# The last pass's inverse deviation: a table value with a Newton step on ScalarE, or a power on GpSimd

## The chip, the cores and the metric

The kernel runs on one core of a Trainium2 chip. A core has a matrix engine (TensorE, PE in the profile; its weight loads are PEld), a vector engine (VectorE, DVE), a scalar engine with function tables (ScalarE, ACT), a general engine (GpSimd, POOL), and a queue engine that issues DMAs (SyncE, SP). Each runs its own instruction stream in order; semaphores tie the streams together. On-chip memory is SBUF, with 128 partitions; matmul results land in PSUM banks. The metric is the device time of one execution, in microseconds (us).

## The reference

One layer of a hybrid decoder trunk over 1024 tokens (plus 16 prepended ones) of width 1024: input projections, a convolution branch and a windowed attention branch, a gated merge, a layer norm, and then a convolutional feed-forward block with a second layer norm. Only its end matters here:

```python
def layer_norm(x, g, b):
    xf = x.astype(jnp.float32)
    mu = xf.mean(-1, keepdims=True)
    var = jnp.square(xf - mu).mean(-1, keepdims=True)
    return ((xf - mu) * lax.rsqrt(var + LN_EPS) * g + b).astype(x.dtype)
...
f = (jax.nn.gelu(g, approximate=False) * u) @ ffn_w_down
return layer_norm(DEEPNORM_ALPHA * h + f, ln2_g, ln2_b)
```

Every token (row) of the result needs the mean and the variance of its 1024 values, and one inverse deviation, 1/sqrt(var + 1e-5).

## The kernel before

The down projection is the last stage. Its output is 1024 tokens by 1024 columns, cut into eight row tiles of 128 tokens and two column halves of 512; matrix products are done in seven passes over half-size blocks, each pass accumulating four PSUM banks (`down`, L1735 and after). A pass's `done` function takes each finished bank into the row tiles `rows[i]` in SBUF. The first six passes finish row tiles 4 to 7 and the second halves of tiles 0 to 3. The seventh, `down(X, True, c11_, 5)` at L1876, finishes the first half of tiles 0 to 3, one tile after another: with `by_tile=5` all remaining operands of a tile are multiplied before the next tile's, so the tiles become ready one by one. Tile 3 comes in two parts of 256 columns, in two banks.

`c11_` (L1850) is what happens to each of these tiles. On VectorE: the bank is added to the row (L1858), the half's statistics are taken (L1859), and both halves' statistics are joined to a mean and a variance, `mv` (L246, in `ln_stats`). Then the inverse deviation `r_` is made. Then each of the row's two halves is centred and multiplied by the gain, `(r - mu) * g2` (L1865), and each half is scaled by the inverse deviation and shifted, `r * rs + b2` (L1867); behind each of these a store of 256 KB to the output is issued on SyncE's queue (L1868, through the helper at L113). L1865 does not need the inverse deviation; L1867 does.

The inverse deviation (L253 to L259) is made mainly on ScalarE: a table value of 1/sqrt(var + eps) (L253), its square (L257), that square times `t_` plus 1.5 (L258), and the product with the table value (L259): one Newton step. `t_` is -0.5 (var + eps), a small VectorE instruction (L256). The `pin` argument is given by `c11_` alone; every other user of `ln_stats` makes its Newton step on VectorE (L261 to L263).

The order of work is planned: the program is laid out with a simulated schedule and ranks, and `after(a, b)` fixes an order between two instructions of an engine by hand. `pin_tail` (L1845) strings all VectorE instructions of `c11_` in the written order, so that tile i's two L1867 stand before tile i+1's L1858. GpSimd and ScalarE instructions of the tail are not strung. GpSimd has one other instruction there, a copy of six columns of statistics for tile 3 (L1857).

The constants used are small tiles filled by VectorE at the start of the program: `eps` (L173), `half` and `three_half` (L226 and L227).

Of the kernel before, what the change touches and what calls it, by code (L numbers as in the profile page):

```python
# [23 lines left out]
F = mybir.dt.float32  # L24
R = mybir.dt.float32r
AF = mybir.ActivationFunctionType
OP = mybir.AluOpType
AX = mybir.AxisListType

P = 128  # L30
# [18 lines left out]
EPS = 1e-5  # L49
# [52 lines left out]
def tile_hybrid_layer(  # L102
# [3 lines left out]
    nc = tc.nc  # L106
# [15 lines left out]
    def after(ins, first):  # L122

        tc.add_manual_dep(ins.ins, first.ins.name, mybir.DependencyInfo(
            mybir.DependencyClass.NoSync, mybir.DependencyReason.SCHED_ONLY), reason="order of work")
# [10 lines left out]
    const = ctx.enter_context(tc.tile_pool(name="const", bufs=1, side="left"))  # L136
# [34 lines left out]
    eps = const.tile([P, 1], F, name="eps")  # L171
# [52 lines left out]
    half_2 = const.tile([P, 2], F, name="half")  # L224
    half_, three_half = (half_2[:, i:i + 1] for i in range(2))
    nc.vector.memset(half_, 0.5)  # L226
    nc.vector.memset(three_half, 1.5)  # L227
    nc.vector.memset(xm[:NMETA], 0.0)
    nsink = const.tile([P, NH], F, name="nsink")

    def ln_stats(srcs, pool=None, tag="", bufs=4, behind=None, half_stats=None, pin=None):

        pool = pool or small
        J = len(srcs)
        n = max(n for _, n in srcs)
        mv = pool.tile([P, J, 2], F, name="mv", tag="mv" + tag, bufs=bufs)
        if any(m < n for _, m in srcs):
            nc.vector.memset(mv, 1.0)
        for j, (src, m) in enumerate(srcs):
            st = half_stats or small.tile([P, 2, 6], F, name="st")  # L240
            for i in range(0 if half_stats is None else 2, 2):
                ins = nc.vector.bn_stats(st[:m, i, :], src[:, i * 512:(i + 1) * 512])
                if behind is not None:
                    after(ins, behind)
                    behind = None
            ins = nc.vector.bn_aggr(mv[:m, j], st[:m].rearrange("p a b -> p (a b)"))  # L246
            if pin:
                pin(ins)
        sd = pool.tile([P, 2, J], F, name="sd", tag="sd" + tag, bufs=bufs)
        t_, r_ = (sd[:n, i] for i in range(2))  # L250
        var = mv[:n, :, 1]

        nc.scalar.activation(r_, var, AF.Abs_reciprocal_sqrt, bias=eps[:n], scale=1.0)  # L253
        if pin:
            sq = pool.tile([P, J], F, name="sq")
            pin(nc.vector.tensor_scalar(t_, var, EPS, -0.5, OP.add, OP.mult))  # L256
            nc.scalar.activation(sq, r_, AF.Copy, scale=r_)  # L257
            nc.scalar.activation(sq, sq, AF.Identity, scale=t_, bias=three_half)  # L258
            nc.scalar.activation(r_, r_, AF.Copy, scale=sq)  # L259
            return [(mv[:m, j, 0:1], r_[:m, j:j + 1]) for j, (_, m) in enumerate(srcs)]  # L260
        nc.vector.scalar_tensor_tensor(t_, var, EPS, r_, OP.add, OP.mult)  # L261
        nc.vector.scalar_tensor_tensor(t_, t_, -0.5, r_, OP.mult, OP.mult)
        nc.vector.scalar_tensor_tensor(r_, t_, 1.5, r_, OP.add, OP.mult)  # L263
        return [(mv[:m, j, 0:1], r_[:m, j:j + 1]) for j, (_, m) in enumerate(srcs)]
# [409 lines left out]
    bias = ap.tile([P, 2, NH // 2, KW], F, name="bias")  # L674
# [318 lines left out]
    def pin(ins):  # L993

        if pinned:
            after(ins, pinned[-1])
        pinned.append(ins)
# [321 lines left out]
    def out_rows(i, between=(), work=()):  # L1319
# [40 lines left out]
        with rank(RK_TURN):  # L1360
            (mu, rs), = ln_stats([(r, n)], half_stats=st if n == P else None)
            for a in (512, 0) if i == 5 else (None,):
                x = r if a is None else r[:, a:a + 512]
                ins = pin(nc.vector.tensor_scalar(x, x, mu, rs, OP.subtract, OP.mult))
# [462 lines left out]
    def norm_out(t):  # L1827
        r, (g2, b2_) = rows[t], gains[2:]
        (mu, rs), = ln_stats([(r, P)], half_stats=stats[t])
        for half in range(2):  # L1830
            hs = slice(half * 512, half * 512 + 512)
            a = r[:, hs]
            nc.vector.scalar_tensor_tensor(a, a, mu, g2[:, hs], OP.subtract, OP.mult)
            nc.vector.scalar_tensor_tensor(a, a, rs, b2_[:, hs], OP.mult, OP.add)
            load(out[0, t * P:(t + 1) * P, hs], a)
# [14 lines left out]
    def c11_(i, part=1):  # L1850
        r, (g2, b2_) = rows[i], gains[2:]
        cs, bank = slice(0, 512), X[i]
        if i == 3:
            cs, bank = slice(part * 256, part * 256 + 256), (X[3], Z[3])[part]
            if part == 0:
                old, stats[3] = stats[3], dn.tile([P, 3, 6], F, name="st3x")
                nc.gpsimd.tensor_copy(stats[3][:, 2], old[:, 1])  # L1857
        pin_tail(nc.vector.tensor_tensor(r[:, cs], r[:, cs], bank[:, cs], OP.add))  # L1858
        pin_tail(nc.vector.bn_stats(stats[i][:, part if i == 3 else 0], r[:, cs]))  # L1859
        if i == 3 and part == 0:  # L1860
            return
        (mu, rs), = ln_stats([(r, P)], half_stats=stats[i], pin=pin_tail)
        halves = [slice(h * 512, h * 512 + 512) for h in range(2)]
        for hs in halves:
            pin_tail(nc.vector.scalar_tensor_tensor(r[:, hs], r[:, hs], mu, g2[:, hs], OP.subtract, OP.mult))  # L1865
        for hs in halves:
            pin_tail(nc.vector.scalar_tensor_tensor(r[:, hs], r[:, hs], rs, b2_[:, hs], OP.mult, OP.add))  # L1867
            load(out[0, i * P:(i + 1) * P, hs], r[:, hs])  # L1868
# [62 lines left out]
```

## Time and profile before

| | |
|---|---|
| median of 3 runs | 1236.19 us (1235.96 to 1236.53) |
| span of the profiled execution, first to last instruction | 1234.6 us |
| TensorE busy | 1225.2 us (99%) |
| VectorE busy | 1085.2 us (88%) |
| ScalarE busy | 584.7 us (47%) |
| GpSimd busy | 15.6 us (1%), 20 instructions |
| granted TensorE clock, mean | 0.999 |

The profile describes one execution; the page gives its span and no other time of it, and the median is that of runs timed by themselves. A row of the timeline reads: start in us, length in us, engine, source line, operation, output<-inputs by the program's names, their shapes, and how many instructions are merged into the row; in square brackets the idle time of the engine before it and what ended it. The chain is the work that ended last, followed back from the end, with start, length, engine, output and line. A row of groups reads: line, engine, operation, names, shapes and count, then busy us and mean ns of one, then idle us before them and what ended the idle time. A row of one line's instructions gives their shortest, median and longest duration in ns, and the first and last start.

### The profile page before, as it was taken

How to read it: one execution, taken by the hardware profiler on the slowest of the kernel's cores; microseconds unless marked ns; L12 is line 12 of the kernel's file. 1: busy time of each engine (PE TensorE's matmuls, PEld its weight loads, DVE VectorE, ACT ScalarE, POOL GpSimd, SP SyncE). 2: the span in 40 equal slices, each digit the busy share in tenths (PEclk: the TensorE clock that was granted, in tenths of full speed). 3: DMA queues.
4: the chain of work that ended last, by engine and by line, in shares of the span. 5: the costliest groups of instructions: out<-in, count | busy, mean ns of one | idle time of the engine just before them, and what ended most of it. 6: DMA issues, size and time to landing. Idle time of an engine off the chain costs nothing.

```text
span 1234.6 us, 21810 instructions
## 1 busy us (share of the span) xinstructions
PE 1225.2 (99%) x8568; PEld 1141.5 (92%) x8568; DVE 1085.2 (88%) x1842; ACT 584.7 (47%) x1065; POOL 15.6 (1%) x20
## 2 busy tenths in 40 slices
PE   9999999999999999999999999999999999999997
PEld 8999989999999999888999999999999998888886
DVE  8899989999879798659899999998999986996697
ACT  7532336654255223345755545555455554445331
POOL 1000000000000010000000000000000000000000
PEclk9999999999999999999999999999999999999999
DMA  7396834412255655322255555554455568988722
GB/s 282 74 298 151 210 98 116 127 55 73 82 158 163 183 140 144 104 85 87 66 171 207 191 187 205 188 183 142 172 203 190 178 239 304 391 315 312 256 86 85
DMA packets 109152, 213.02 MB, mean 173 GB/s; under 512 B 31883, under 2 KB 46779, under 8 KB 108922
## 3 DMA queue, kind: packets, MB, share of 16 engines
q1 hardware_dynamic: 93050, 200.56, 49.5%
q10 hardware_dynamic: 16000, 11.07, 2.9%
q8 instruction: 67, 1.10, 0.4%
q14 instruction: 35, 0.29, 0.1%
HBM read 149.98 MB, written 62.70 MB: 172 GB/s over the span
## 4 chain that ended last, share of the span: by engine, by line
PE 98%; DVE 1%; ACT 0%; issue 0%; DMA 0%; POOL 0%; DVEq 0%; POOLq 0%
PE px L1599 14%; PE py L1599 9%; PE ps_x L1745 9%; PE ps_z L315 8%; PE ps_z L314 8%; PE ps_z L310 8%; PE ps_z L1745 8%; PE pw L1599 5%; PE pz L1599 5%; PE ps_p L310 2%; PE ps_p L314 2%; PE ps_p L315 2%; PE ps_w L310 2%; PE ps_w L315 2%; PE ps_w L314 2%; PE ps_z L550 2%
## 5 line engine op out<-in xcount | busy, mean ns | idle before, releaser
L707 DVE SCALAR_TENSOR_TENSOR FA<-cin,cols,FA 128x1026 f32<-128x1026 f32 x120 | 152.2, 1277 | 0.9
L315 PE MATMUL ps_z<-RHO,wlo 128*128 128x256 f32 (+2 forms) x324 | 103.5, 320 | 0.0
L314 PE MATMUL ps_z<-RHO,whi 128*128 128x256 f32 (+2 forms) x324 | 103.4, 319 | 0.0
L315 PE MATMUL ps_z<-RHC,wlo 128*128 128x256 f32 (+2 forms) x324 | 103.4, 319 | 0.0
L314 PE MATMUL ps_z<-RHC,whi 128*128 128x256 f32 (+2 forms) x324 | 103.4, 319 | 0.0
L310 PE MATMUL ps_z<-RHO,whi 128*128 128x256 f32 (+2 forms) x324 | 103.3, 319 | 0.0
L310 PE MATMUL ps_z<-RHC,whi 128*128 128x256 f32 (+2 forms) x324 | 103.2, 319 | 0.0
L279 ACT CAST whi<-wr 128x1024 fp32r<-128x1024 f32 x37 | 38.9, 1050 | 107.4 <-PE ps_z L314 85.5
L1408 ACT CAST RHO<-wr 128x512 fp32r<-128x512 f32 x92 | 55.3, 619 | 25.3 <-DVE wr L1426 11.7
L1409 DVE TENSOR_TENSOR RHO<-wr,RHO 128x512 fp32r<-128x512 f32 x92 | 61.8, 684 | 5.1 <-ACT RHO L1408 5.0
L310 PEld LDWEIGHTS ps_z<-RHO,whi 128*128 128x128 f32 x324 | 60.9, 188 | 4.3
L314 PEld LDWEIGHTS ps_z<-RHO,whi 128*128 128x128 f32 x324 | 61.0, 188 | 4.2
L310 PEld LDWEIGHTS ps_z<-RHC,whi 128*128 128x128 f32 x324 | 60.9, 188 | 4.1
L314 PEld LDWEIGHTS ps_z<-RHC,whi 128*128 128x128 f32 x324 | 61.0, 188 | 4.0
L315 PEld LDWEIGHTS ps_z<-RHO,wlo 128*128 128x128 f32 x324 | 60.9, 188 | 4.0
L315 PEld LDWEIGHTS ps_z<-RHC,wlo 128*128 128x128 f32 x324 | 61.0, 188 | 3.9
L1426 DVE TENSOR_TENSOR wr<-wr 128x512 f32<-128x512 f32 x88 | 59.9, 681 | 0.2
L282 DVE TENSOR_TENSOR wlo<-wr,whi 128x1024 fp32r<-128x1024 f32 x35 | 42.7, 1220 | 11.8 <-ACT whi L279 11.4
L1611 ACT COPY FA<-px 128x514 f32<-128x514 f32 (+2 forms) x23 | 13.2, 572 | 70.7 <-PE px L1599 70.6
L1408 ACT CAST ws<-wr 128x512 fp32r<-128x512 f32 x60 | 36.1, 618 | 18.8 <-DVE wr L1426 10.7
L714 ACT ACTIVATE FA<-ps_z,cols 128x258 f32<-128x258 f32 (+2 forms) x48 | 26.1, 544 | 39.4 <-PE ps_z L315 36.6
L1599 PE MATMUL px<-OA,RHO 128*128 128x258 f32 (+1 forms) x336 | 43.8, 279 | 0.0
(491 smaller groups left out, 3488.2 us busy)
## 6 DMA issues: line engine op xcount, KB each, us to landing
wr<-in_w_up_dram SPq DMA_DIRECT2D x44, 512.0 KB, 4.6
wr<-in_w_z_dram SPq DMA_DIRECT2D x30, 512.0 KB, 3.9
fd<-FA SPq DMA_DIRECT2D x44, 256.0 KB, 2.4
OB<-in_w_down_dram SPq DMA_DIRECT2D x19, 512.0 KB
qt<-qd SPq DMA_DIRECT2D x28, 256.0 KB, 4.1
td<-OB SPq DMA_DIRECT2D x12, 512.0 KB
sums<-fd SPq DMA_DIRECT2D x12, 512.0 KB, 7.6
sd<-sums SPq DMA_DIRECT2D x12, 512.0 KB
```

The source lines that it names most:

```text
L279: ins = nc.scalar.copy(hi, raw)
L282: return (nc.vector if quick else nc.gpsimd).tensor_tensor(lo, raw, f32(hi), OP.subtract)
L310: ins = nc.tensor.matmul(ps, ah, bh, start=i == 0, stop=False)
L314: nc.tensor.matmul(ps, ah, bl, start=False, stop=False)
L315: last = nc.tensor.matmul(ps, al, bh, start=False, stop=i == n - 1)
L707: nc.vector.scalar_tensor_tensor(acc[c], cin[:, j:j + U], wc, acc[c], OP.mult, OP.add)
L714: nc.scalar.activation(t, ps, AF.Tanh, bias=bcol(14 + i), scale=0.5)
L1408: nc.scalar.copy(hi, src)
L1409: ins = nc.vector.tensor_tensor(lo, src, f32(hi), OP.subtract)
L1426: ins = nc.vector.tensor_tensor(*x)
L1599: ins = nc.tensor.matmul(o, x[:, ks], bmat(sub, q, hl, k), start=first and k + j == 0, stop=k == 3 and j == 2, skip_group_check=not first)
L1745: nc.tensor.matmul(bank[:, cs], l[:, ts], r[:, ws], start=first and a and x + k == 0, stop=z and x == len(ops) - 1 and k == 2, skip_group_ ...
```

## The change

In the last pass (where `pin` is given) the table value, the VectorE instruction for `t_` and the three ScalarE instructions go. In their place GpSimd adds eps to the variance, and then raises the sum to the power of -0.5, with a second input tile that holds -0.5. That tile, `mhalf`, is a new constant of 128x1, filled by VectorE at the start. Every other user of `ln_stats` keeps its instructions. The two new instructions are not in the hand-written order.

```diff
     nc.vector.memset(half_, 0.5)
+    mhalf = const.tile([P, 1], F, name="mhalf")
+    nc.vector.memset(mhalf, -0.5)
     nc.vector.memset(three_half, 1.5)
...
-        nc.scalar.activation(r_, var, AF.Abs_reciprocal_sqrt, bias=eps[:n], scale=1.0)
-        if pin:
-            sq = pool.tile([P, J], F, name="sq")
-            pin(nc.vector.tensor_scalar(t_, var, EPS, -0.5, OP.add, OP.mult))
-            nc.scalar.activation(sq, r_, AF.Copy, scale=r_)
-            nc.scalar.activation(sq, sq, AF.Identity, scale=t_, bias=three_half)
-            nc.scalar.activation(r_, r_, AF.Copy, scale=sq)
+        if not pin:
+            nc.scalar.activation(r_, var, AF.Abs_reciprocal_sqrt, bias=eps[:n], scale=1.0)
+        else:
+            nc.gpsimd.tensor_scalar(t_, var, EPS, None, OP.add)
+            nc.gpsimd.tensor_tensor(r_, t_, mhalf, OP.pow)
             return [(mv[:m, j, 0:1], r_[:m, j:j + 1]) for j, (_, m) in enumerate(srcs)]
```

## The prediction

> **What bounds the kernel now.** I read the page's head and its chain first, then the chain in order of time over the last 35 us, then the timeline of that stretch.
>
> ```profile
> span 1234.6 us, 21810 instructions
> PE 1225.2 (99%) x8568; PEld 1141.5 (92%) x8568; DVE 1085.2 (88%) x1842; ACT 584.7 (47%) x1065; POOL 15.6 (1%) x20
> PE 98%; DVE 1%; ACT 0%; issue 0%; DMA 0%; POOL 0%; DVEq 0%; POOLq 0%
> ```
>
> TensorE (PE) is the bound for 98% of the chain. The change touches only what comes after the last matmul, and three row tiles just before it. The chain in order of time shows that end:
>
> ```profile
> 1223.42 3.97 PE ps_z L1745 x33
> ...
> 1228.40 0.25 DVE mv L246
> 1228.65 0.02 issue
> 1228.67 0.30 ACT sd L253
> ...
> 1229.00 0.30 ACT sq L257
> ...
> 1229.33 0.40 ACT sq L258
> ...
> 1229.75 0.30 ACT sd L259
> ...
> 1230.08 0.75 DVE r L1867
> ```
>
> The last matmul ends at 1223.42 + 3.97 = 1227.39. From there the end is a string of small instructions; the four of ScalarE (ACT) stand in it, from 1228.67 to 1230.05. So the chain says that 1.4 us of ACT work are on the path. The timeline of VectorE (DVE) corrects this:
>
> ```profile
> 1212.48 0.69 DVE L1858 TENSOR_TENSOR r<-r,ps_x 128x512 f32<-128x512 f32 x1 [3.74 <-PE ps_x L1745]
> ...
> 1213.93 0.21 DVE L246 BATCH_NORM_AGGREGATE mv<-st 128x2 f32<-128x12 f32 x1
> ...
> 1215.57 1.41 DVE L1867 SCALAR_TENSOR_TENSOR r<-r,sd,b 128x512 f32<-128x512 f32 x2
> 1216.90 0.68 DVE L1858 TENSOR_TENSOR r<-r,ps_x 128x512 f32<-128x512 f32 x1
> ...
> 1226.19 0.43 DVE L1859 BATCH_NORM_STATS2 st3x<-r 128x6 f32<-128x256 f32 x1
> 1227.41 0.42 DVE L1858 TENSOR_TENSOR r<-r,ps_z 128x256 f32<-128x256 f32 x1 [0.79 <-PE ps_z L1745]
> ...
> 1228.40 0.24 DVE L246 BATCH_NORM_AGGREGATE mv<-st3x 128x2 f32<-128x18 f32 x1
> 1228.67 0.15 DVE L256 TENSOR_SCALAR sd<-mv 128x1 f32<-128x1 f32 x1
> 1228.74 1.41 DVE L1865 SCALAR_TENSOR_TENSOR r<-r,mv,g 128x512 f32<-128x512 f32 x2
> 1230.08 1.41 DVE L1867 SCALAR_TENSOR_TENSOR r<-r,sd,b 128x512 f32<-128x512 f32 x2
> ```
>
> Three things are to be seen. First, while ACT works, DVE runs the two centring instructions of L1865; the second would let the next start at 1228.74 + 2 x 0.67 = 1230.08, where L1867 does start (0.67 is half the distance from 1228.74 to 1230.08). ACT's four instructions and DVE's own work end within 0.03 us of each other: ACT's chain is fully covered, so its removal alone buys next to nothing. Second, from 1212.48 on DVE runs the first three tiles without a gap (no idle before the second tile's L1858 at 1216.90): there DVE, not PE, sets the pace, and its order is pinned. Third, that run ends in one gap of 0.79 us, before the 1227.41 row, where DVE waits for the last matmul. That gap is the only slack: delay of the first three tiles beyond 0.79 us in all reaches the end, delay of the last tile reaches it whole.
>
> **The change part by part.** Per tile, four ACT instructions and one DVE instruction (L256) go. Without L256, the first L1865 starts at 1228.67 in place of 1228.74, a gain of 0.07; the pair then ends at 1228.67 + 1.41 = 1230.08, and L1867 could start at 1230.01. In the first three tiles this only lengthens the 0.79 gap. So the best case is -0.07 us.
>
> What is added is two GpSimd (POOL) instructions of 128x1, an addition and then the power, between the same two DVE instructions. Their prices come from the groups of POOL by line and form and from the timeline of the start:
>
> ```profile
> L423 POOL TENSOR_SCALAR t<-mv 128x1 f32<-128x1 f32 x1 | 0.2, 192 | 0.1
> L430 POOL TENSOR_SCALAR t<-t,r 128x1 f32<-128x1 f32 x1 | 0.3, 343 | 1.1 <-ACT r L417 1.1
> L282 POOL TENSOR_TENSOR wlo<-wr,whi 128x1024 fp32r<-128x1024 f32 x2 | 4.9, 2454 | 42.1 <-ACT whi L279 42.1
> 4.42 0.20 DVE L412 BATCH_NORM_AGGREGATE mv<-st 32x2 f32<-32x12 f32 x1
> 4.71 0.18 POOL L423 TENSOR_SCALAR t<-mv 32x1 f32<-32x1 f32 x1 [1.39 <-DVE mv L412]
> 5.90 0.26 POOL L433 TENSOR_SCALAR m<-mv,t 32x1 f32<-32x1 f32 x1
> 6.19 0.81 ACT L466 ACTIVATE xm<-xm,m,t 32x512 f32<-32x512 f32 x1 [1.25 <-POOL m L433]
> 7.50 0.34 POOL L430 TENSOR_SCALAR t<-t,r 128x1 f32<-128x1 f32 x1 [1.06 <-ACT r L417]
> 7.94 0.27 POOL L431 TENSOR_SCALAR t<-t,r 128x1 f32<-128x1 f32 x1
> ```
>
> Addition: the same form as L423, 0.19. Waking POOL from DVE's aggregate: 4.62 to 4.71, 0.09. Between dependent POOL instructions: 7.84 to 7.94, 0.10. Waking the consumer: 6.16 to 6.19, 0.03. The power p is in no row. Its floor is the cheapest 128x1 row, 0.19; as an upper end I take the dearest thing of its form in the trace, the two-input instruction over 1024 columns, 2.45. Between ends that far apart I price it as two of the dearest 128x1 row (a power is more than one arithmetic step): 2 x 0.343 = 0.69, which is also close to the geometric middle of the ends (0.68).
>
> POOL and DVE do not run freely beside each other. The timeline where POOL last had large work shows it, with the undisturbed lengths from the rows of those two lines:
>
> ```profile
> 441.00 0.42 DVE L1192 SCALAR_TENSOR_TENSOR RHO<-OB,RHO 128x256 fp32r<-128x256 f32 x1
> 441.19 2.53 POOL L282 TENSOR_TENSOR RX<-FA,RX 128x1024 fp32r<-128x1024 f32 x1 [432.62 <-DMA OB<-sgd]
> 441.34 2.66 DVE L1192 SCALAR_TENSOR_TENSOR RHC<-OB,RHC 128x256 fp32r<-128x256 f32 x1
> 451.71 1.28 DVE L1146 SCALAR_TENSOR_TENSOR two<-FA,pair,two 128x1024 f32<-128x1024 f32 x1
> 452.01 3.24 POOL L282 TENSOR_TENSOR RW<-OB,RW 128x1024 fp32r<-128x1024 f32 x1 [8.29 <-DMA OB<-sgd]
> 452.91 0.42 DVE L1184 SCALAR_TENSOR_TENSOR OB<-OB,ps_p 128x258 f32<-128x258 f32 x1
> L1192 DVE SCALAR_TENSOR_TENSOR RHC<-OB,RHC x14: 410/419/2661, 420.7 to 500.4; 128x256 fp32r<-128x256 f32 x14
> ```
>
> A DVE instruction with two SBUF inputs (L1192) that meets a running POOL instruction takes 2.66 in place of 0.42; one with a PSUM input (L1184, 0.42) does not notice. It holds the other way too: the POOL instruction that began during L1146 took 3.24 in place of 2.45. POOL does get its turn between two such DVE instructions: at 441.19 it was let in ahead of the second L1192. The hand-over comes a little before the recorded end: 444.00 - 0.42 = 443.58 against POOL's end at 443.72 (0.14 early); 455.25 - 2.45 = 452.80 against DVE's end at 452.99 (0.19 early). L1865 reads r and g2, both in SBUF, so it is of this kind.
>
> The last tile, then. The aggregate ends at 1228.64. DVE starts the first L1865 at 1228.67, ahead of POOL, which wakes at 1228.73 and is held until 1228.67 + 0.75 - 0.19 = 1229.23 (0.75 being 1.41 less the 0.67 spacing). The addition ends at 1229.42 and gives the port back at 1229.28, in time for the second L1865 at 1229.34, which is not delayed. The power is issued at 1229.52, finds that one running, and is held until 1230.08 - 0.19 = 1229.89. It ends at 1229.89 + 0.69 = 1230.58, and L1867 starts at 1230.61 in place of 1230.08: +0.53 per tile, or in general p - 0.16. Behind L1867 wait, on DVE, the next tile's L1858 and all after it, and on SyncE's queue the two stores of the tile.
>
> In the first tile the distance from aggregate to L1867 is the same (1214.14 to 1215.57, 1.43, against 1.44), so three tiles add 3 x 0.53 = 1.59, of which the gap takes 0.79: +0.80. The last adds 0.53. Sum +1.33 us. The stores that follow move with L1867 at their present price. No PE instruction waits for any of this: no matmul is left after 1227.39.
>
> Here a rule decides what the rows leave open, whether so small a POOL instruction is held too. The Trainium skill, page "SBUF — State Buffer", section "Who interferes with whom", says that a DVE instruction with two SBUF inputs contends with any GpSimd instruction that reads SBUF, and that the second to issue is blocked until the first is through. The 2.66 and 3.24 above agree with it, for 128x1024 only; by the rule the sum is +1.33, without it -0.07.
>
> Edits costed at nothing. The new DVE memset of 128x1 and the column it fills:
>
> ```profile
> 0.99 0.06 DVE L227 MEMSET half<- 128x1 f32 x1
> 3.11 1.27 DVE L411 BATCH_NORM_STATS2 st<-xm 32x6 f32<-32x512 f32 x2 [0.98 <-DMA xm<-in_meta_tokens_dram]
> ```
>
> 0.06 us, covered by DVE's 0.98 us wait for the first load; bare it would cost 0.06. POOL's queue holds one more thing in the tail, the copy of L1857 (six columns), wanted only by the last aggregate; ACT and its queue have nothing else there.
>
> **The rivals.**
> *The power is slow (slower).* Mechanism and place as above, price p. The sum is 4(p - 0.16) - 0.79, which passes +2.47 us (0.2%) at p = 0.98; at p = 1.6 it is +5.0 (1241.2), at the upper end 2.45 it is +8.4 (1244.6). [...] Against: 128x1 rows are all at 0.19 to 0.34.
> *Hidden anyway.* If so small an instruction does not wait for the port, the addition runs 1228.73 to 1228.92, the power from 1229.02 to 1229.71, and L1867 starts when DVE is free: -0.07, 1236.1, as long as p is under 0.96. For it: no row shows a 128x1 POOL instruction held. Against: the rows above.
> *First use costs a load.* ACT shows such a thing:
>
> ```profile
> 0.74 1.28 ACT L174 ACT_TABLE_LOAD   x1 [0.74 <-PEq L1920]
> ```
>
> If the first power pays 1.28 as well, the first tile is later by that much, the gap is used up already, and the sum is 1.33 + 1.28 = +2.61, 1238.8. Against: POOL's first two-input row (2.53) is hardly longer than a later one's 2.45. The Trainium skill, "GPSIMD Engine Reference", section "Instruction dispatch", gives some 6 us for the first call of a freshly loaded GpSimd kernel; by that figure the sum would be an estimated +7.3. No run here shows it.
> *The order of the rest moves.* The order is planned from a simulated schedule, and all tiles behind the new column may shift in SBUF. What it could gain is bounded: PE is idle 1234.6 - 1225.2 = 9.4 us, of which 1234.6 - 1227.4 = 7.2 lie after the last matmul; the 2.2 left are under 0.2%. It could as well lose as much, or more.
>
> **How the numbers follow.** 0.2% (2.47 us) is about what a measurement of this kernel can tell from no change. Chances: forecast (port held, p up to 0.98, 1236.2 to 1238.7) 0.43; hidden 0.12; slow power 0.29; load at first use 0.08; order moves 0.03 for the better, 0.05 for the worse. Within 0.2%: 0.43 + 0.12 = 0.55; slower: 0.29 + 0.08 + 0.05 = 0.42; faster: 0.03. The span of 1234.6 lies 1.6 below the runs' median of 1236.19, which I take as what lies around the span and unchanged: 1236.19 + 1.33 = 1237.5 (span 1235.9). The range runs from 1236.0, just under the hidden case, to 1243.0, which is p = 2.06; some 0.05 is left out below and 0.1 above.
>
> **What would show it.** ACT empty after 1212; per tile a POOL addition whose row is stretched beyond 0.19 by the first L1865, and a power that ends after the second; DVE idle before the first L1867 of each tile, put down to POOL, of some 0.6 us (1230.01 to 1230.61); L1865 still at 0.75. The gap of 0.79 gone. The prediction is wrong if the power's own time is over 1 us, if the first tile alone is late, if POOL ends before the second L1865 does, or if times before 1212 have moved.

## The result, and the profile after

The changed kernel takes 1249.77 us (1249.67 to 1249.82) against 1236.19: a ratio of 1.011, 95% interval 1.0097 to 1.0123, slower by 13.6 us. The head of its page:

```profile
span 1247.9 us, 21794 instructions
PE 1237.9 (99%) x8568; PEld 1149.9 (92%) x8568; DVE 1085.5 (87%) x1839; ACT 579.8 (46%) x1049; POOL 22.3 (2%) x28
```

The first surprise is in the PE figure: 1237.9 us busy where it was 1225.2, with the same 8568 matmuls. The change doesn't touch one of them. The timeline of VectorE (DVE) says where the time lies relative to the last pass. These are the first row tile and the last one of the changed kernel:

```profile
1224.78 0.69 DVE L1858 TENSOR_TENSOR r<-r,ps_x 128x512 f32<-128x512 f32 x1 [4.12 <-PE ps_x L1745]
...
1226.48 1.42 DVE L1865 SCALAR_TENSOR_TENSOR r<-r,mv,g 128x512 f32<-128x512 f32 x2
1228.36 1.41 DVE L1867 SCALAR_TENSOR_TENSOR r<-r,sd,b 128x512 f32<-128x512 f32 x2 [0.47 <-POOL sd L259]
...
1240.27 0.40 DVE L1858 TENSOR_TENSOR r<-r,ps_z 128x256 f32<-128x256 f32 x1
...
1241.17 0.24 DVE L248 BATCH_NORM_AGGREGATE mv<-st3x 128x2 f32<-128x18 f32 x1
1241.44 1.42 DVE L1865 SCALAR_TENSOR_TENSOR r<-r,mv,g 128x512 f32<-128x512 f32 x2
1243.31 1.41 DVE L1867 SCALAR_TENSOR_TENSOR r<-r,sd,b 128x512 f32<-128x512 f32 x2 [0.45 <-POOL sd L259]
```

Everything the prediction was about lies from the first of these rows on. That row was at 1212.48 and is now at 1224.78: 12.3 us are lost before the changed code runs at all. From there to the end of the span it was 22.12 us and is 23.12: the changed part itself costs 1.0 us. It does so in the way foretold: DVE waits 0.45 to 0.47 us for GpSimd (POOL) ahead of each L1867, and the gap ahead of the last tile's L1858 (1240.27) is gone.

For the 12.3 us, the instructions of two lines give the time of their first and last matmul, with shortest, median and longest duration in ns. Before, then after:

```profile
L1599 PE MATMUL px<-OA,RHO x336: 276/278/375, 603.3 to 1013.1; 128*128 128x258 f32 x84, 128*128 128x256 f32 x84
L1745 PE MATMUL ps_z<-OC,RHC x108: 283/389/395, 1017.3 to 1225.3; 128*128 128x512 f32 x96, 128*128 128x256 f32 x12
```

```profile
L1599 PE MATMUL px<-OA,RHO x336: 276/282/389, 605.5 to 1022.0; 128*128 128x258 f32 x84, 128*128 128x256 f32 x84
L1745 PE MATMUL ps_z<-OC,RHC x108: 277/395/397, 1026.2 to 1237.6; 128*128 128x512 f32 x96, 128*128 128x256 f32 x12
```

The delay is 2.2 us at the start of the up projection (603.3 to 605.5), 8.9 at its end, and 12.3 at the end of the down projection (1225.3 to 1237.6). It is no stall but a steady loss. The groups by line and form show which matmuls lose. Before:

```profile
L1599 PE MATMUL px<-OC,RHO 128*128 128x256 f32 x312 | 39.6, 276 | 0.0
L1745 PE MATMUL ps_x<-OC,RHO 128*128 128x512 f32 x144 | 33.1, 389 | 0.0
L1599 PE MATMUL px<-RHC,RHO 128*128 128x256 f32 x168 | 21.4, 276 | 0.0
L1745 PE MATMUL ps_x<-RHC,RHO 128*128 128x512 f32 x72 | 17.5, 389 | 0.0
```

After:

```profile
L1599 PE MATMUL px<-OC,RHO 128*128 128x256 f32 x312 | 41.2, 281 | 0.0
L1745 PE MATMUL ps_x<-OC,RHO 128*128 128x512 f32 x144 | 34.1, 396 | 0.0
L1599 PE MATMUL px<-RHC,RHO 128*128 128x256 f32 x168 | 21.3, 276 | 0.0
L1745 PE MATMUL ps_x<-RHC,RHO 128*128 128x512 f32 x72 | 17.5, 390 | 0.0
```

Matmuls that read OC and RHO went from 276 to 281 ns and from 389 to 396; those that read RHC and RHO did not move. The two kinds differ in one thing. One operand of a matmul is the weights, which the weight-load (PEld) rows bring in; the other is the moving operand. Tiles are stacked in SBUF from two sides: the constants, RHC and RHO from the left, OC and RX from the right. In the built programs the new constant of 4 bytes takes 32 bytes per partition, so everything on the left behind it moves by 32 (RHC from 53184 to 53216) and nothing on the right does (OC stays at 196032). The order of instructions on PE and on the SyncE queue is the same in both programs. The theory after the result is therefore: the power costs the tail 1 us, and the column costs the rest, because it changes the distance in memory between the two operands of a matmul. Not every row fits: some matmuls with both operands on the left slowed a little too (px<-OA,RHO of 128x256 from 276 to 279); experiments 3 and 4 come back to that.

### The profile page after: what moved, and what is told of

It is laid out like the page before. It is cut to its first block, busy times and chain, and to the rows that moved or that the text cites. A ratio compares the mean times of both kernels' runs of the same rounds, so it can differ in the third digit from the quotient of the medians.

```text
span 1247.9 us, 21794 instructions
## 1 busy us (share of the span) xinstructions
PE 1237.9 (99%) x8568; PEld 1149.9 (92%) x8568; DVE 1085.5 (87%) x1839; ACT 579.8 (46%) x1049; POOL 22.3 (2%) x28
## 4 chain that ended last, share of the span: by engine, by line
PE 96%; DVE 2%; POOL 1%; ACT 0%; issue 0%; DMA 0%; POOLq 0%; DVEq 0%
PE px L1599 15%; PE py L1599 10%; PE ps_x L1745 9%; PE ps_z L315 8%; PE ps_z L314 8%; PE ps_z L310 8%; PE ps_z L1745 7%; PE pz L1599 5%; PE pw L1599 5%; PE ps_p L310 2%; PE ps_p L315 2%; PE ps_p L314 2%; PE ps_w L310 2%; PE ps_w L314 2%; PE ps_w L315 2%; PE ps_z L550 2%
## 5 line engine op out<-in xcount | busy, mean ns | idle before, releaser
L315 PE MATMUL ps_z<-RHO,wlo 128*128 128x256 f32 (+2 forms) x324 | 103.4, 319 | 0.0
L310 PE MATMUL ps_z<-RHO,whi 128*128 128x256 f32 (+2 forms) x324 | 103.4, 319 | 0.0
L310 PE MATMUL ps_z<-RHC,whi 128*128 128x256 f32 (+2 forms) x324 | 103.4, 319 | 0.0
L315 PE MATMUL ps_z<-RHC,wlo 128*128 128x256 f32 (+2 forms) x324 | 103.3, 319 | 0.0
L310 PEld LDWEIGHTS ps_z<-RHO,whi 128*128 128x128 f32 x324 | 60.9, 188 | 4.4
L315 PEld LDWEIGHTS ps_z<-RHO,wlo 128*128 128x128 f32 x324 | 61.0, 188 | 4.1
L310 PEld LDWEIGHTS ps_z<-RHC,whi 128*128 128x128 f32 x324 | 60.9, 188 | 4.1
L315 PEld LDWEIGHTS ps_z<-RHC,wlo 128*128 128x128 f32 x324 | 61.0, 188 | 3.9
L1409 DVE TENSOR_TENSOR ws<-wr,ws 128x512 fp32r<-128x512 f32 x60 | 40.4, 684 | 6.3 <-ACT ws L1408 6.3
```

The lines of the kernel that those rows point to most:

```text
L310: ins = nc.tensor.matmul(ps, ah, bh, start=i == 0, stop=False)
L315: last = nc.tensor.matmul(ps, al, bh, start=False, stop=i == n - 1)
L1409: ins = nc.vector.tensor_tensor(lo, src, f32(hi), OP.subtract)
```

## The experiments

**1. The power without the column.** The value -0.5 takes the place of 1.5, which nothing reads any more:

```diff
-    mhalf = const.tile([P, 1], F, name="mhalf")
-    nc.vector.memset(mhalf, -0.5)
-    nc.vector.memset(three_half, 1.5)
+    nc.vector.memset(three_half, -0.5)
...
-            nc.gpsimd.tensor_tensor(r_, t_, mhalf, OP.pow)
+            nc.gpsimd.tensor_tensor(r_, t_, three_half, OP.pow)
```

> The power on GpSimd as in the change, but -0.5 stands in the column that held 1.5, so no tile moves in SBUF. Layout theory (the new column shifts the tiles behind it by 32 bytes and the matmuls that read one shifted and one unshifted operand run slower; the power itself costs only the tail): 1236.2 + 4 x 0.46 - 0.79 = 1237.3 us, matmuls of 128x256 back at 113 ns apart, first addition of the last pass at 1212.5 us in the trace. Rival (the GpSimd work itself, or the planner's answer to it, slows the matmuls): 1249 to 1250 us, the first addition at about 1224.8.

Measured: 1237.07 us (1236.93 to 1237.29) against 1236.16, ratio 1.0008, interval 0.9998 to 1.0017. The head of its page, the first addition of the last pass, and the last tile:

```profile
PE 1224.7 (99%) x8568; PEld 1141.0 (92%) x8568; DVE 1084.9 (88%) x1838; ACT 579.9 (47%) x1049; POOL 22.4 (2%) x28
1212.16 0.69 DVE L1856 TENSOR_TENSOR r<-r,ps_x 128x512 f32<-128x512 f32 x1 [3.75 <-PE ps_x L1743]
...
1228.55 0.24 DVE L246 BATCH_NORM_AGGREGATE mv<-st3x 128x2 f32<-128x18 f32 x1
1228.82 1.42 DVE L1863 SCALAR_TENSOR_TENSOR r<-r,mv,g 128x512 f32<-128x512 f32 x2
1230.69 1.42 DVE L1865 SCALAR_TENSOR_TENSOR r<-r,sd,b 128x512 f32<-128x512 f32 x2 [0.45 <-POOL sd L257]
```

(This kernel is two lines shorter: its L1856, L1863 and L1865 are L1858, L1865 and L1867 of the kernel before.) PE is back at 1224.7 us with the GpSimd work in place. The rival (GpSimd or the planner slows the matmuls) falls. The interval takes in 1, so the +0.9 us does not rest on the times alone: each of the four tiles shows a wait for GpSimd like the 0.45 us of the last row (0.45 to 0.47).

**2. The column without the power.** The kernel before, with the two added lines for `mhalf` and nothing else.

> The kernel before, with the new column and its memset and nothing else of the change. Layout theory: 1236.2 + 12.3 = 1248.5 us, and the tail from the first addition of the last pass to the end unchanged at 22.1 us. Rival (the power or the planner slows the matmuls): 1236.2 us, within 0.3.

Measured: 1248.97 us (1248.93 to 1249.05), +12.8 us, ratio 1.0103, interval 1.0088 to 1.0119. From the first addition of the last pass (1224.96) to the end of the span (1247.1) it takes 22.1 us, as the kernel before does. With experiment 1 that accounts for the whole: 12.8 + 0.9 = 13.7 against 13.6. A constant that nobody reads costs 1%.

**3 and 4. Which move is harmful.** In one the change has a tile of 64 bytes in place of 32; in the other the kernel before has the column on the left and a second one at the outer end of the right-hand tiles:

```diff
-    mhalf = const.tile([P, 1], F, name="mhalf")
+    mhalf = const.tile([P, 16], F, name="mhalf")[:, :1]
```

```diff
+    rpad_p = ctx.enter_context(tc.tile_pool(name="rpad", bufs=1, side="right"))
     qsp_stack = ExitStack()
...
+    mhalf = const.tile([P, 1], F, name="mhalf")
+    nc.vector.memset(mhalf, -0.5)
+    rpad = rpad_p.tile([P, 1], F, name="rpad")
+    nc.vector.memset(rpad, 0.0)
```

> The change with a column tile of 64 bytes in place of 32, so that everything behind it moves by 64. If the 64-byte phase between a matmul's two operands is what counts: 1237.3 us, as without the column. If any move of the left-hand tiles against the right-hand ones costs the same: 1249.8. If the cost grows with the distance: above 1250.

> The kernel before, with the new column on the left and a second one of 32 bytes at the outer end of the right-hand tiles, so that both groups of tiles stand at 32 modulo 64. If the phase between the two operands counts: 1236.2 us, within 1. If the absolute place counts (operands off a 64-byte line are slow): 1248.5 us or more, since the right-hand operands are off the line too.

Measured: 1253.81 us (+17.7; ratio 1.0146, interval 1.0129 to 1.0163) and 1253.11 us (+16.9; 1.0137, 1.0122 to 1.0152). My guess, that only the remainder of the distance by 64 bytes counts (the 64-byte phase), was wrong in both. But the two agree with each other: the right-hand tiles are stacked downwards, so the second column there moves them down by 32 (OC from 196032 to 196000), and the distance between left and right changes by 32 + 32 = 64 bytes, as in the first; less the 0.9 us of the power the first is +16.8. The rival that operands off a 64-byte line are slow falls as well: in the first of the two all these tiles stand on such a line. What counts is the distance between the two groups, not where each stands, and its period is longer than 64 bytes. Sorting the matmuls of these traces by the distance between their operands pointed to 256: in the last stage a 128x512 matmul starts some 227 ns after the one before at remainder 0, and 233 at 32, 192 or 224.

The 64-byte kernel also holds something that the distance alone doesn't explain:

```profile
L1599 PE MATMUL px<-OC,RHO 128*128 128x256 f32 x312 | 41.3, 282 | 0.0
L1599 PE MATMUL px<-RHC,RHO 128*128 128x256 f32 x168 | 22.1, 281 | 0.0
```

Here the matmuls with both operands on the left went from 276 to 281 as well, although the distance between those two had not changed. The order of work in the same trace says more:

```profile
643.13 1.52 PE L1599 MATMUL pw<-RHC,ws 128*128 128x256 f32 x12
644.49 1.59 PE L1599 MATMUL py<-RX,ws 128*128 128x256 f32 x12
645.92 1.58 PE L1599 MATMUL py<-OC,ws 128*128 128x256 f32 x12
647.34 1.58 PE L1599 MATMUL px<-OA,ws 128*128 128x256 f32 x12
648.75 1.58 PE L1599 MATMUL px<-RHC,ws 128*128 128x256 f32 x12
650.17 1.58 PE L1599 MATMUL py<-OA,RHO 128*128 128x256 f32 x12
```

The first and the fifth row both read RHC and ws, two tiles on the left. From its start to the next row's the first takes 1.36 us, 113 ns a matmul. The fifth takes 1.42, 118 ns, where the kernel before takes 1.36 for either. The fifth stands behind rows of RX and OC, whose distance did change. So the slow pace carries over to matmuls behind whose own distance is unchanged. In the kernel with the change it dies out sooner: px<-OA,ws in this place takes 1.40 us, and px<-RHC,ws behind it 1.36. No run tests this by itself; the order of the rows shows it.

**5 and 6. One group of operands alone.** In the kernel before, only the places in OC of the last stage are moved, by 8 columns (32 bytes) or by 64 (256 bytes):

```diff
-    W_DN = [(OC, 0), (OC, 2048), (OC, 4096), (OC, 6144), (RHC, 2048), (RHC, 4096), (RHO, 6144)]
+    W_DN = [(OC, 8), (OC, 2056), (OC, 4104), (OC, 6152), (RHC, 2048), (RHC, 4096), (RHO, 6144)]
```

> The kernel before, with one group of operands of the last stage (the four places in OC) moved by 8 columns, 32 bytes, and nothing else. If the distance between a matmul's two operands is what counts: the 510 matmuls of 128x512 that read OC against RHC, RHO or RX go from 389 ns to about 395 a row, 510 x 6.2 = +3.2 us, 1239.4; those that do not read OC stay at 389. If the earlier cost came from something else that a new column moves (constants, small tiles, DMAs): 1236.2.

> The same operands moved by 64 columns, 256 bytes. If the cost depends on the distance modulo 256 bytes, as the sorted matmuls of the six traces suggest: 389 ns again and 1236.2 us. If any move away from the old place costs: 1239 or more. A stall at the start of the stage (the new place overlaps operands of the stage before) may add up to 1 us; the matmul rows stay readable.

Measured: 1239.91 us (ratio 1.003, interval 1.0019 to 1.0041) and 1236.20 us (1.0001, 0.9991 to 1.001). The groups of the first, then of the second:

```profile
L1599 PE MATMUL px<-OC,RHO 128*128 128x256 f32 x312 | 39.6, 276 | 0.0
L1745 PE MATMUL ps_x<-OC,RHO 128*128 128x512 f32 x144 | 34.1, 395 | 0.0
```

```profile
L1745 PE MATMUL ps_x<-OC,RHO 128*128 128x512 f32 x144 | 33.1, 389 | 0.0
```

This is the decisive pair. No tile moves; 32 bytes inside one tile cost 6 ns for each 128x512 matmul that reads them (389 to 395) and +3.7 us in all, where +3.2 was expected; the stage before, which is not moved, keeps its 276. 256 bytes cost nothing. One thing these runs can't separate: the weights of neighbouring matmuls mostly lie 512 or 4096 bytes apart, multiples of 256, so the distance that counts may be that to a matmul's own weights or to the next one's, which are loaded beside it (PEld is busy for 92% of the span and PE for 99%).

**7. The centring off the port.** The port is the access to SBUF for which VectorE and GpSimd wait on each other in the prediction. The power without the column, with the bank in PSUM in place of the gain, so that the gain is left out of the last four tiles:

```diff
-            pin_tail(nc.vector.scalar_tensor_tensor(r[:, hs], r[:, hs], mu, g2[:, hs], OP.subtract, OP.mult))
+            pin_tail(nc.vector.scalar_tensor_tensor(r[:, hs], r[:, hs], mu, X[0], OP.subtract, OP.mult))
```

> The power without a new column, with the centring instructions of the last pass reading a PSUM bank in place of the gain, so the gain is left out of the last four tiles. A PSUM input takes VectorE off the port it shares with GpSimd. If the two GpSimd instructions were held by the centring (port): the addition falls from 0.77 to 0.19 us and the power from 0.92 to about 0.52, VectorE does not wait for GpSimd, and the distance from aggregate to L1865 falls from 1.90 to about 1.4 us; time about 1236.1. If 0.77 and 0.92 are their own lengths: rows unchanged, L1865 still late by 0.46, 1237.1.

Measured: 1235.93 us, ratio 0.9997, interval 0.9987 to 1.0008. GpSimd in the last tile, first in experiment 1 and then here:

```profile
1228.88 0.77 POOL L256 TENSOR_SCALAR sd<-mv 128x1 f32<-128x1 f32 x1 [3.38 <-DVE mv L246]
1229.73 0.92 POOL L257 TENSOR_TENSOR sd<-sd,half 128x1 f32<-128x1 f32 x1
```

```profile
1228.38 0.21 POOL L256 TENSOR_SCALAR sd<-mv 128x1 f32<-128x1 f32 x1 [4.88 <-DVE mv L246]
1228.68 0.56 POOL L257 TENSOR_TENSOR sd<-sd,half 128x1 f32<-128x1 f32 x1
```

With no DVE instruction of two SBUF inputs beside them, the addition takes 0.21 in place of 0.77 and the power 0.56 in place of 0.92. The difference, 0.56 and 0.36, is waiting for the port. The power's own price is 0.56 us.

**8. The addition on VectorE, the power alone on GpSimd.** Again without the column, and with the gain:

```diff
-            nc.gpsimd.tensor_scalar(t_, var, EPS, None, OP.add)
+            pin(nc.vector.tensor_scalar(t_, var, EPS, None, OP.add))
```

> The power without a new column, with eps added on VectorE just ahead of the centring and only the power on GpSimd. Port theory with a power of 0.52 of its own: held by the first centring instruction, then it holds up the second by about 0.35, so L1865 comes 0.35 later than in the kernel before (0.46 with both on GpSimd); 4 x 0.35 - 0.79 = +0.6, 1236.8 us. If the power takes 0.92 by itself: it runs from 0.4 us after the aggregate, ends 1.3 us after it, and VectorE waits only for the port.

Measured: 1236.07 us, ratio 0.9998, interval 0.9988 to 1.0009. I expected 1236.8, so the step from both instructions to one is worth more than I thought: no cost is left that the interval would show. The last tile:

```profile
1228.36 0.15 DVE L256 TENSOR_SCALAR sd<-mv 128x1 f32<-128x1 f32 x1
1228.43 1.40 DVE L1863 SCALAR_TENSOR_TENSOR r<-r,mv,g 128x512 f32<-128x512 f32 x2
1229.75 1.41 DVE L1865 SCALAR_TENSOR_TENSOR r<-r,sd,b 128x512 f32<-128x512 f32 x2
1228.59 0.99 POOL L257 TENSOR_TENSOR sd<-sd,half 128x1 f32<-128x1 f32 x1 [4.63 <-DVE sd L256]
```

The power is held (0.99 against 0.56), but it ends at 1229.58, before DVE is free at 1229.75, and nobody waits. The pair of centring instructions takes 1.40, as in the kernel before: the second starts at 1229.09, while the power is at work (its last 0.56 us, if its own work comes last, run from 1229.02), and is not held up. So in this order GpSimd does not keep the port through the power. The likely reading, not shown by itself, is that it needs the port only while it reads its operands. One trip to GpSimd fits beside the centring; two do not, because each is held by one of the two centring instructions.

**9 and 10. The same distance in the first stage.** If distance is the rule everywhere, the first stage (L310 to L315) should have room: its distance is 64 bytes modulo 256. One kernel moves its input by 16 columns to a distance of 0; the other moves it to 192 and cuts the group of 512 columns into two of 256:

```diff
-        o = 6196 + i * 272 if a < 272 else 16 + i * 768 - 272
+        o = 6196 + i * 272 if a < 272 else i * 768 - 272
```

```diff
-ZG = [(0, 272), (272, 528), (528, 1040)]
+ZG = [(0, 272), (272, 528), (528, 784), (784, 1040)]
...
-        o = 6196 + i * 272 if a < 272 else 16 + i * 768 - 272
+        o = 6196 + i * 272 if a < 272 else 48 + i * 768 - 272
```

> The kernel before, with the first stage's input (h0, the moving operand of the 128x256 and 128x512 matmuls at L310 to L315) moved by 16 columns, so that its distance from the weights is 0 modulo 256 bytes in place of 64. If distance is the rule in this stage too: the 648 matmuls of 128x512 go from 231.4 to about 226.7 ns apart (-3.0 us), the 648 of 128x256 from 116.3 to about 119.9 (+2.3 us, from the few at that distance in the last stage); together about -0.7 us, 1235.5. If the rule is one of the two later stages only: 1236.2 and both spacings unchanged.

> The kernel before, with the same input moved the other way, to a distance of 192 bytes modulo 256, and the 512-column group of that stage cut into two of 256, since 128x256 ran 113.8 ns apart at 192 and 128x512 did not do well there. Distance rule: per weight block 3 x 113.8 = 341.4 ns in place of 116.3 + 231.4 = 347.7, 648 times: -4.1 us, 1232.1, unless the 50% more evacuations and waits of that stage take it back. Rival (the spacing is not set by distance here): 1236.2 or more, since 648 matmuls and their evacuations are added.

Measured: 1238.29 us (ratio 1.0017, interval 1.0008 to 1.0026) and 1242.05 us (1.0049, 1.0032 to 1.0066); both slower, where a gain was expected. Groups of the kernel before, then of the first of the two, then of the second:

```profile
L315 PE MATMUL ps_z<-RHO,wlo 128*128 128x512 f32 x108 | 42.5, 394 | 0.0
L315 PE MATMUL ps_z<-RHO,wlo 128*128 128x256 f32 x108 | 30.1, 279 | 0.0
```

```profile
L315 PE MATMUL ps_z<-RHO,wlo 128*128 128x512 f32 x108 | 42.2, 391 | 0.0
L315 PE MATMUL ps_z<-RHO,wlo 128*128 128x256 f32 x108 | 30.7, 284 | 0.0
```

```profile
L310 PE MATMUL ps_z<-RHO,whi 128*128 128x256 f32 x324 | 90.9, 281 | 2.4 <-ACT FA L714 1.3 <-DVE cin L698 1.1
```

Distance does act here too: at 0 the 128x256 matmuls went from 279 to 284, as expected. But the 128x512 ones gained 3 ns at best in place of 5, and the sum came out at +2.1. At 192 the 128x256 matmuls did not come down to the 276 of the later stage (279 to 281 in the six groups), so the cut brought 648 more matmuls and 2.4 us of waits in this row for nothing. The means of one stage did not carry over to another. From one start to the next, the median 128x256 matmul of this stage took 114 ns before and 114 at 192, and two of them take as long as the median one of 512 columns did (229): there was next to nothing to gain. Why the others in this stage are slower than the median stays open. No version clearly faster than the kernel before was found.

## Why the prediction was wrong

- **What bounds the kernel: right.** TensorE; and for that very reason a change to each matmul of a few ns outweighs the whole tail.
- **"Edits costed at nothing": this step failed.** I priced the new memset of 128x1 "and the column it fills" at 0.06 us at most. The memset is covered as foretold. The column measured 12.8 us (experiment 2), through matmuls that run 5 to 7 ns slower. I had asked what the instruction costs and not what the tile displaces. The last of the prediction's signs of being wrong is the one that came: times before 1212 have moved, by 12.3 us at the last pass.
- **The rival "the order of the rest moves": right in kind, without a price.** It named tiles shifting in SBUF and gave it 0.05 for the worse with "as much, or more" than 2.2 us as its only number; the range ended at 1243.0, the price of a slow power. Its bound on a gain, PE's idle 2.2 us, took PE's busy time as fixed, and that rose from 1225.2 to 1237.9. The order itself did not move on PE. No row of the trace of before gives the price of a move, but there were hints: matmuls of one form ran at different speeds in different stages (128x512 at 394 ns in L315 and 389 in L1745), and the kernel keeps two tiles that nothing reads, pad_c (L970) and pad_a (L973), a sign that the places of the tiles behind them had been chosen. Nor could one see it by the side of SBUF: OC,RHO and RHC,RHO ran equally fast, at 276 and 276 ns.
- **The tail: right in mechanism, a little high.** Forecast +1.33 us; +0.9 without the column (experiment 1). DVE waits 0.45 to 0.47 per tile in place of 0.60; the scaling (L1867, there L1865) starts 1.90 after the aggregate's end in experiment 1 (1228.79 to 1230.69), where it was 1.44, so 0.46 late in place of 0.53; 4 x 0.46 - 0.79 = 1.05. The gap of 0.79 is gone, as foretold.
- **Its terms.** The power: 0.69 forecast, 0.56 measured (experiment 7). The addition: 0.19 forecast, 0.21 measured, and its row stretched to 0.77 by the first centring (0.69 foretold). Waking GpSimd, 0.09 in the forecast, shows as 0.08 in the chain. The hold of the power: 0.37 forecast (1229.52 to 1229.89), 0.36 measured.
- **The rule taken from the Trainium skill**, page "SBUF — State Buffer", section "Who interferes with whom", that any GpSimd instruction that reads SBUF contends with a DVE instruction of two SBUF inputs: the trace agrees for 128x1, with 0.77 against 0.21 us. That the second is blocked until the first is through holds for GpSimd behind DVE; it did not hold for DVE behind the power (experiment 8).
- **The other rivals.** "Hidden anyway" fell: both instructions were held. "The power is slow" fell: 0.56 is under the 0.98 where it would have decided. "First use costs a load" fell: the first power took as long as the last in the changed kernel, as these two rows show. Both hold a wait for the port; without one, in experiment 7, the first took 0.58 and the last 0.56.

```profile
1227.40 0.93 POOL L259 TENSOR_TENSOR sd<-sd,mhalf 128x1 f32<-128x1 f32 x1
...
1242.35 0.92 POOL L259 TENSOR_TENSOR sd<-sd,mhalf 128x1 f32<-128x1 f32 x1
```

## What to carry to other kernels

A new tile, however small, is a change to every tile behind it: in a kernel bound by TensorE, keep the layout when you test an idea (put a constant into a tile that is there), and test the layout by itself. If the first changed instruction is late already, and PE is busy longer with the same matmuls, compare matmul groups of one shape by the tiles they read before explaining anything else. Look at the order too: a slow group can slow the one behind it. Work sent to GpSimd beside VectorE instructions with two SBUF inputs waits once for each instruction that it sends; one such trip was hidden here, two in a row were not.

## What the runs showed of the hardware

- The time of a matmul depends on where its two operands lie relative to each other. Moving one of them by 32 bytes took 128x512 matmuls from 389 to 395 ns and the kernel from 1236.2 to 1239.9; moving it by 256 took them back to 389 and 1236.2.
- A slow pace carries over: in the 64-byte kernel matmuls whose own distance had not changed took 113 ns each ahead of slowed ones and 118 behind them.
- Open ends: in the first stage the same distances brought other gains than in the later ones. Which resource is behind it, whether a matmul's own weights or the next one's count, and which distance is best for which shape, was not settled.
- A power of 128x1 takes 0.56 us on GpSimd, and an addition 0.21. Neither kept VectorE waiting for the port in these traces; in experiment 1 VectorE kept both of them waiting, by 0.56 (the addition) and 0.36 (the power).
